# One encoder layer on one core: the small tables of the Fourier branch and of the rotation are loaded and split some column blocks later, and the first sum of folded weights is queued behind a low part on VectorE

## The chip, the core and the metric

The kernel runs on one core of a Trainium2 chip. Five engines work side by side, each through its own queue in order: TensorE (PE, matrix products and transposes; PEld is its load of the stationary operand), VectorE (DVE), ScalarE (ACT), GpSimd (POOL) and SyncE (SP), which here only issues transfers from and to main memory. The metric is the device time of one execution in microseconds, as the median of several runs.

## What is computed

One layer of a bidirectional encoder, 256 positions of 2048 channels, everything in float32:

```python
h = x + 0.5 * rms_post(swiglu(rms_pre(x)))            # first feed-forward half, width 5632
u = rms_pre(h);  q, k, v, f, g = split(u @ w_in)      # one projection for all of them
y_attn = gqa(rope(rms(q)), rope(rms(k)), v) @ w_attn_o   # 16 query heads, 4 key heads, 2-D rotation
y_four = real(fft2(f by groups of 128 channels)) @ w_fourier
merged = sigmoid(g_A) * y_attn + sigmoid(g_B) * y_four
h = h + rms_post(merged @ w_out)
y = h + 0.5 * rms_post(swiglu(rms_pre(h)))            # second half, same form
```

## The kernel before, in words

**Products in three passes.** Each float32 operand is split into a high part (a copy on ScalarE that rounds to the fast format, L104) and a low part (the difference, on VectorE, L105) by the helper `split` (L103). A product is three passes of TensorE: high by high (L110), high by low and low by high (L111, L112). So each weight goes through one ScalarE and one VectorE instruction before TensorE can use it. `split` notes the last two instructions that it made in `latest["A"]` and `latest["V"]`.

**How weights come.** A weight piece is 128 x 1024 elements (512 KB). It is loaded into one of 5 raw buffers (tag `raw`), split into one of 6 pairs of ring buffers (tags `hi`, `lo`), and used by 12 products: two blocks of 128 rows, two groups of 128 channels, three passes. Other small things share 8 buffers of the tag `wk`: temporary blocks, the rotation tables, the raw tables of the Fourier branch (`draw`, `mraw`), the gate bias `bg`, the sums `z`. Three buffers of the tag `xt` hold `z2` (sums of the Fourier branch), two tables (`alt`, `mid`), and later `acc` and `nraw`.

**Column blocks.** `col_block(u, w_in, nb, between, at)` computes 512 columns of the projection in 16 steps kk (one group of 128 channels each, 6 products per step), in four groups of two pieces. The entries of `between` are spread evenly: with n entries, entry i is called at the first step at or above (i + 1) * 16 / (n + 1). What it puts on TensorE is queued behind the product just made; its work on other engines isn't bound to that place.

**What sets the order.** The program is written once from top to bottom; the queue of each engine is then laid out when the program is built. An instruction is placed when a planner's estimate says that its inputs and its buffer are ready, earlier program text first. So a load or a split can be put well ahead of where it stands in the text. In the region of `last_rows` (the seam of two layers) the order on VectorE is written by hand among its own instructions. `tc.issue_after(ins)` puts what is written inside it, as far as it is on the engine of `ins`, behind `ins` in that engine's queue; it is an order, not a wait.

**The seam.** `last_rows` ends the first feed-forward half and begins the mixers: it adds the normed result to `h` (L405), multiplies by the next gain (L418, written `y`), transposes blocks of four (L180), splits them, and computes block 4 of `w_in` (the keys) between. Behind it, in program text, stand the loads of the rotation tables (`gq`, `gk`, `rc`, `rsn`) and of six tables of the Fourier branch: `dps` (256 positions, 128 x 258), `dcs` (channels, 128 x 256), `odd`, `first`, `alt`, `mid`; the first two are split, the other four are copied.

**The mixers.** Then follow in text: block 5 (values), gate 10, block 0 (first queries), gates 11, 12 and 13 (each a column block, a bias and a sigmoid). `fold_tokens` (L876) mirrors the token blocks with the row roots from `finish`, and `fold_f` (L932) takes 16 pieces of the Fourier projection during blocks 0, 11, 12, 13. `tables` (L831) multiplies the rotation tables by the gains; `norm_rope` uses them from gate 10 on. In gate 6 `fourier_positions` (`zh`, `zl`, reads `odd` and `dps`) and `fourier_channels` (reads `dcs`, `mid`, `alt`) come between steps, then `turn_q` for both blocks of queries. `fourier_weights(cb)` (L1106) takes four weight pieces: it adds two halves in the raw buffer (L1118), forms a difference (L1119), splits both, and sums a row over the four in `acc` (L1126, L1128), with factors from `fourier_channels`. `fourier_out` multiplies them (`pf`), after the attention scores (`sc`) and before the parts of attention.

Of the kernel before, what the change touches and what calls it, by code (L numbers as in the profile page):

```python
# [2 lines left out]

# [1 line left out]

# [10 lines left out]
ALU = mybir.AluOpType  # L16
# [42 lines left out]
def encoder_layer(  # L59
# [24 lines left out]
    def load(dst, src):  # L84
        nc.sync.dma_start(dst, src)
# [4 lines left out]
    def work(name, shape=None):  # L90
        return wk.tile(shape or [P, NB], F32, tag="wk", name=name)
# [11 lines left out]
    def split(hi, lo, src):  # L103
        a = A.activation(hi, src, AF.Copy)  # L104
        v = V.tensor_tensor(out=lo, in0=src, in1=hi.bitcast(F32), op=ALU.subtract)  # L105
        latest["A"], latest["V"] = a.ins, v.ins
# [714 lines left out]
        load(spill[t], h[t][:])  # L821

    gq, gk = work("gq", [P, HD]), work("gk", [P, HD])
    load(gq[:], q_g.partition_broadcast(P))
    load(gk[:], k_g.partition_broadcast(P))
    rc, rsn = work("rc", [P, NT, HD]), work("rsn", [P, NT, HD])
    load(rc[:], rope_cos)
    load(rsn[:], rope_sin)
    tabs = {}

    def tables():  # L831
        for nm, g in (("q", gq), ("k", gk)):
# [59 lines left out]
        ts = slice(t * P, (t + 1) * P)  # L892
        transpose4(kro[t], kT[:, 0, :, ts], kT[:, 1, :, ts])

    def constant(src, n):
        raw = work("draw", [P, n])
        load(raw[:], src)
        return raw

    WE, WO = P + 2, P  # L900
    dps = const.tile([P, 2, WE + WO], F32R, name="dps")
    split(dps[:, 0, :], dps[:, 1, :], constant(dft_pos, WE + WO)[:])
    dcs = const.tile([P, 2, 2 * P], F32R, name="dcs")
    split(dcs[:, 0, :], dcs[:, 1, :], constant(dft_ch, 2 * P)[:])
    odd = const.tile([P, WE], F32R, name="odd")
    A.activation(odd[:], constant(dft_ones[:, 0:WE], WE)[:], AF.Copy)
    first = const.tile([P, P], F32R, name="first")
    A.activation(first[:], constant(dft_ones[:, WE:WE + P], P)[:], AF.Copy)
    alt = xpool.tile([P, GROUPS // 2, NYR], F32R, tag="xt", name="alt")
    A.activation(alt[:].rearrange("p a b -> p (a b)"), constant(dft_ones[:, WE + P:], GROUPS // 2 * NYR)[:], AF.Copy)  # L910
    mid = xpool.tile([NS, 2 * P + 2 * NYR], F32R, tag="xt", name="mid")
    mraw = work("mraw", [NS, 2 * P + 2 * NYR])
    load(mraw[:], dft_mid)
    A.activation(mid[:], mraw[:], AF.Copy)


    fs, fraw = [], {}
# [80 lines left out]
    def fourier_channels(b, i, a):  # L998

        (ah, al), (oh, ol) = a  # L1000
        j = 2 * b + i
        if j == 0:
            foT.append(new_chunk("foT"))
            pmid[0] = ptr.tile([P, NB], F32, tag="tr", name="pn")
        pb = ptr.tile([P, NB], F32, tag="tr", name="pb")
        c = slice(i * WO, (i + 1) * WO)
        mm3(pb[:, 0:WO], dcs[0:PO, 0, P:2 * P], dcs[0:PO, 1, P:2 * P], oh[0:PO, c], ol[0:PO, c], True, True)
        c, m, o = slice(i * WE, (i + 1) * WE), slice(2 * WE, 3 * WE), pb[:, WO:WO + WE]
        mm3(o, dcs[0:PO, 0, 0:P], dcs[0:PO, 1, 0:P], ah[0:PO, c], al[0:PO, c], True, False)
        T.matmul(o, mid[:, i * P:(i + 1) * P], ah[0:NS, m], start=False, stop=False)  # L1010
        T.matmul(o, mid[:, i * P:(i + 1) * P], al[0:NS, m], start=False, stop=True)
        o = pmid[0][0:NYR, 0:WE]
        T.matmul(o, alt[0:PO, j, :], ah[0:PO, c], start=j == 0, stop=False)
        T.matmul(o, alt[0:PO, j, :], al[0:PO, c], start=False, stop=False)
        if i == 1:
            n = slice(2 * P + b * NYR, 2 * P + (b + 1) * NYR)
            T.matmul(o, mid[:, n], ah[0:NS, m], start=False, stop=False)
            T.matmul(o, mid[:, n], al[0:NS, m], start=False, stop=b == 1)
        split(foT[0][0][:, j, :], foT[0][1][:, j, :], pb[:, 0:2 * P])
        A.activation(dcol[:, j:j + 1], pb[:, 2 * P:2 * P + 1], AF.Copy)  # L1020
        if j == 3:
            A.activation(mids[0:NYR, :], pmid[0][0:NYR, 0:P], AF.Copy)
            V.tensor_tensor(out=mids[64:NYR, :], in0=pmid[0][64:NYR, 0:P], in1=mids[64:NYR, :].bitcast(F32), op=ALU.subtract)
            A.activation(dcol[0:GROUPS, 4:5], pmid[0][0:GROUPS, P:P + 1], AF.Copy)
# [69 lines left out]
    def gate(nb, dst, cb, between=(), at=()):  # L1094

        ps = col_block(u, w_in, nb, between=between, at=at)
        bg = work("bg")
        load(bg[:], b_gate[:, (nb - 6) * NB:(nb - 5) * NB].partition_broadcast(P))
        for t in range(NT):
            z = work("z")  # L1100
            V.scalar_tensor_tensor(out=z[:], in0=ps[t][:], scalar=rs[t][:, 0:1], in1=bg[:], op0=ALU.mult, op1=ALU.add)
            A.activation(cbs(dst[t], cb), z[:], AF.Sigmoid)
# [3 lines left out]
    def fourier_weights(cb):  # L1106


        acc = xpool.tile([P, NB], F32, tag="xt", name="acc")
        nraw, wn = xpool.tile([P, NB], F32, tag="xt", name="nraw"), workr("wn")  # L1110
        load(nraw[0:NYR, :], w_fn[cb])
        A.activation(wn[0:NYR, :], nraw[0:NYR, :], AF.Copy)
        V.tensor_tensor(out=wn[32:40, :], in0=nraw[32:40, :], in1=wn[32:40, :].bitcast(F32), op=ALU.subtract)
        forms = []
        for j in range(4):
            raw = wraw.tile([P, 2, NB], F32, tag="raw", name="raw")
            load(raw[:], w_fo[cb, j].rearrange("p (k c) -> p k c", k=2))
            V.tensor_tensor(out=raw[:, 0, :], in0=raw[:, 0, :], in1=raw[:, 1, :], op=ALU.add)  # L1118
            V.scalar_tensor_tensor(out=raw[:, 1, :], in0=raw[:, 1, :], scalar=-2.0, in1=raw[:, 0, :],  # L1119
                                   op0=ALU.mult, op1=ALU.add)  # L1120
            hi = wring.tile([P, 2, NB], F32R, tag="hi", name="whi")
            lo = wring.tile([P, 2, NB], F32R, tag="lo", name="wlo")
            split(hi[:], lo[:], raw[:])
            forms.append((hi, lo))
            if j == 0:
                V.tensor_scalar(out=acc[:], in0=raw[:, 0, :], scalar1=dcol[:, j:j + 1], scalar2=None, op0=ALU.mult)  # L1126
            else:
                V.scalar_tensor_tensor(out=acc[:], in0=raw[:, 0, :], scalar=dcol[:, j:j + 1], in1=acc[:],  # L1128
                                       op0=ALU.mult, op1=ALU.add)
        ready[cb] = acc, nraw, wn, forms  # L1130
# [21 lines left out]
            V.tensor_tensor(out=cbs(mB[t], cb), in0=w[:], in1=cbs(mB[t], cb), op=ALU.mult)  # L1152


    pv = col_block(u, w_in, 5, between=[nxt.finish, tables, lambda: fold_tokens(0)])
    for t in range(NT):
        vt = work("vt")
        A.activation(vt[:], pv[t][:], AF.Copy, scale=rs[t][:, 0:1])
# [7 lines left out]
    pq = col_block(u, w_in, 0, at=folds_at(4))  # L1166
    qs = []
    gate(11, mB, 1, at=folds_at(4), between=[lambda t=t: qs.append(norm_rope(pq, "q", t)) for t in range(NT)])
    gate(12, mB, 2, at=folds_at(4), between=[lambda t=t: turn_k(t) for t in range(NT)])
    gate(13, mB, 3, at=folds_at(4))  # L1170

    yA, zA = ([big(f"{n}{t}") for t in range(NT)] for n in ("yA", "zA"))
    mT = []
# [210 lines left out]
```

## Time and profile before

| | |
|---|---|
| median of 3 runs | 2004.93 us (2003.99 to 2006.01) |
| profiled execution | 2006.3 us |
| its span, first to last instruction | 2004.2 us |
| PE busy | 1984.0 us (99%) |
| DVE busy | 1780.1 us (89%) |
| ACT busy | 1301.2 us (65%) |
| mean granted clock of PE | 0.997 |

The profile is of one execution. Times in its rows are microseconds from the start of the span. A row of the timeline has start, duration, engine (SPq is SyncE's issue of transfers), line, operation, output<-input with buffer numbers left out, sizes and count; a bracket at its end gives the idle time before it and what ended it. A row of the windows has a stretch and its length, then busy time and instructions of PE, PEld, DVE, ACT and POOL, then the granted clock of PE (1.00 is full), the share of the transfer engines' time, and GB/s. A row of waits has the waiting engine and instruction, what it waited for, total, times and longest.

### The profile page before, as it was taken

The numbers are of one execution on the slowest core, as the hardware profiler recorded it, in microseconds if no ns is written. First come the engines' busy times: TensorE is split into PE (matmuls) and PEld (weight loads), VectorE is DVE, ScalarE is ACT, GpSimd is POOL, SyncE is SP. The second block draws the span as 40 slices with busy tenths as digits, with TensorE's granted clock in tenths as the row PEclk, the third lists the DMA queues.
The fourth block names the chain that finished last, engine by engine and source line by source line (L and its number), as shares of the span: only waits on it lengthen the run. The fifth ranks groups of instructions, "written<-read, shape, count | busy, mean of one in ns | idle before, by whom it ended". The sixth has DMA issues, their size and how long they took to land.

```text
span 2004.2 us, 25805 instructions
## 1 busy us (share of the span) xinstructions
PE 1984.0 (99%) x9146; PEld 1644.8 (82%) x9146; DVE 1780.1 (89%) x2352; ACT 1301.2 (65%) x1860; POOL 84.5 (4%) x94
## 2 busy tenths in 40 slices
PE   9999999999999999999999999999999999999998
PEld 7888888888888878888888888878888888888886
DVE  6899999999999878886877885878999999999996
ACT  7566766767667756556666564656677766677666
POOL 0000000000000000100000000000000000000002
PEclk9999999999999999999999999999999999999999
DMA  8657766677668796954555557565577766677673
GB/s 319 211 175 240 225 232 199 200 249 228 226 204 275 250 280 201 261 184 138 195 189 188 192 166 277 194 215 194 169 236 231 231 210 208 213 233 229 208 264 126
DMA packets 117585, 434.20 MB, mean 217 GB/s; under 512 B 12840, under 2 KB 18992, under 8 KB 106064
## 3 DMA queue, kind: packets, MB, share of 16 engines
q1 hardware_dynamic: 103888, 411.65, 59.9%
q0 software_dynamic: 13568, 20.91, 6.0%
q8 instruction: 71, 1.16, 0.2%
q14 instruction: 58, 0.48, 0.1%
HBM read 409.44 MB, written 6.29 MB: 207 GB/s over the span
## 4 chain that ended last, share of the span: by engine, by line
PE 90%; DVE 5%; DMA 3%; ACT 1%; issue 1%; SPq 0%; DVEq 0%; ACTq 0%
PE pc L111 18%; PE pc L112 18%; PE pc L110 18%; PE pr L112 10%; PE pr L111 10%; PE pr L110 10%; DVE wlo L105 2%; PE pt L180 1%; DMA raw<-in_f_gu 1%; DMA raw<-in_w_fo 1%; DVE t L582 0%; PE pe L110 0%; PE pe L112 0%; PE pe L111 0%; PE pt L1072 0%
## 5 line engine op out<-in xcount | busy, mean ns | idle before, releaser
L105 DVE TENSOR_TENSOR wlo<-raw,whi 128x1024 fp32r<-128x1024 f32 (+1 forms) x567 | 681.1, 1219 | 96.9 <-ACT whi L104 95.2
L104 ACT ACTIVATE whi<-raw 128x1024 fp32r<-128x1024 f32 (+1 forms) x567 | 585.8, 1052 | 253.7 <-PE pc L112 109.3
L111 PE MATMUL pc<-wlo,fh 128*128 128x512 f32 x738 | 287.3, 389 | 0.0
L112 PE MATMUL pc<-whi,fl 128*128 128x512 f32 x738 | 287.3, 389 | 0.0
L110 PE MATMUL pc<-whi,fh 128*128 128x512 f32 x738 | 287.1, 389 | 0.0
L110 PE MATMUL pc<-whi,uh 128*128 128x512 f32 x688 | 271.7, 395 | 1.5 <-ACT uh L786 1.5
L111 PE MATMUL pc<-wlo,uh 128*128 128x512 f32 x688 | 269.8, 392 | 1.7 <-DVE wlo L105 1.7
L112 PE MATMUL pc<-whi,ul 128*128 128x512 f32 x688 | 269.6, 392 | 0.0
L104 ACT ACTIVATE whi<-t 128x1024 fp32r<-128x1024 f32 (+1 forms) x198 | 171.6, 867 | 139.4 <-DVE t L582 130.8
L582 DVE TENSOR_TENSOR t<-raw 128x512 f32<-128x512 f32 (+1 forms) x252 | 209.1, 842 | 14.1 <-DMA raw<-in_f_gu 10.3
L110 PE MATMUL pr<-whi,hTh 128*128 128x512 f32 x544 | 213.4, 392 | 0.0
L112 PE MATMUL pr<-whi,hTl 128*128 128x512 f32 x544 | 211.8, 389 | 0.0
L111 PE MATMUL pr<-wlo,hTh 128*128 128x512 f32 x544 | 211.7, 389 | 0.0
L105 DVE TENSOR_TENSOR wlo<-t,whi 128x1024 fp32r<-128x1024 f32 (+1 forms) x198 | 193.6, 978 | 13.4 <-ACT whi L104 13.0
L104 ACT ACTIVATE w<-raw 128x1024 fp32r<-128x1024 f32 x144 | 152.0, 1055 | 40.8 <-DVE raw L582 34.7
L105 DVE TENSOR_TENSOR w<-raw,w 128x1024 fp32r<-128x1024 f32 x144 | 175.6, 1219 | 0.0
L111 PEld LDWEIGHTS pc<-wlo,fh 128*128 128x128 f32 x738 | 138.5, 188 | 29.2 <-DVE wlo L105 0.3
L110 PEld LDWEIGHTS pc<-whi,fh 128*128 128x128 f32 x738 | 138.5, 188 | 28.9
L112 PEld LDWEIGHTS pc<-whi,fl 128*128 128x128 f32 x738 | 138.5, 188 | 28.7
L111 PEld LDWEIGHTS pc<-wlo,uh 128*128 128x128 f32 x688 | 129.8, 189 | 28.5 <-DVE wlo L105 3.6
L110 PEld LDWEIGHTS pc<-whi,uh 128*128 128x128 f32 x688 | 129.7, 188 | 28.5 <-ACT uh L786 2.8
L112 PEld LDWEIGHTS pc<-whi,ul 128*128 128x128 f32 x688 | 129.6, 188 | 27.0
(360 smaller groups left out, 3188.4 us busy)
## 6 DMA issues: line engine op xcount, KB each, us to landing
raw<-in_f_down SPq DMA_DIRECT2D x176, 512.0 KB, 5.0
raw<-in_f_gu SPq DMA_DIRECT2D x144, 512.0 KB, 4.8
raw<-in_f_gu SPq DMA_DIRECT2D x72, 1024.0 KB, 7.0
raw<-in_w_in SPq DMA_DIRECT2D x112, 512.0 KB, 4.5
raw<-in_f_up SPq DMA_DIRECT2D x32, 512.0 KB, 4.5
raw<-in_w_ao SPq DMA_DIRECT2D x32, 512.0 KB, 3.8
raw<-in_w_out SPq DMA_DIRECT2D x32, 512.0 KB, 4.5
raw<-in_f_gate SPq DMA_DIRECT2D x31, 512.0 KB, 5.8
```

The costliest lines, as they stand in the source:

```text
L104: a = A.activation(hi, src, AF.Copy)
L105: v = V.tensor_tensor(out=lo, in0=src, in1=hi.bitcast(F32), op=ALU.subtract)
L110: T.matmul(ps, lh, rh, start=first, stop=False, skip_group_check=onto)
L111: T.matmul(ps, lh, rl, start=False, stop=False, skip_group_check=onto)
L112: return T.matmul(ps, ll, rh, start=False, stop=last, skip_group_check=onto)
L180: T.transpose(pt[:, j, :], src[:, j * P:(j + 1) * P], ident[:])
L582: V.tensor_tensor(out=out, in0=a, in1=b, op=ALU.subtract)
```

## The change

The four loads of the rotation tables move into a function `rotation`, called in block 5 as its second entry; `tables` goes from the second to the fifth of now five entries, `fold_tokens(0)` stays third. With five entries the steps are 3 (`finish`), 6 (`rotation`), 8 (`fold_tokens(0)`) and 14 (`tables`), where they were 4 (`finish`), 8 (`tables`) and 12 (`fold_tokens(0)`).

The six Fourier tables are loaded by `ask` and split or copied by `take`: `alt`, `mid`, `first` in gate 12 (steps 8 and 14, behind the two `turn_k`, which go from steps 6 and 11 to 3 and 6), `dps`, `odd`, `dcs` in gate 13 (steps 4 and 12). `alt` and `mid` get their buffers only then.

The sum of the first folded weight piece (L1118, for cb 0 and j 0 alone) is queued on VectorE behind `latest["V"]`. At that place of the text this is the low part that `turn_q` made last in gate 6 (`qTl` of the second block).

```diff
     gq, gk = work("gq", [P, HD]), work("gk", [P, HD])
-    load(gq[:], q_g.partition_broadcast(P))
-    load(gk[:], k_g.partition_broadcast(P))
     rc, rsn = work("rc", [P, NT, HD]), work("rsn", [P, NT, HD])
-    load(rc[:], rope_cos)
-    load(rsn[:], rope_sin)
     tabs = {}
+
+    def rotation():
+        load(gq[:], q_g.partition_broadcast(P))
+        load(gk[:], k_g.partition_broadcast(P))
+        load(rc[:], rope_cos)
+        load(rsn[:], rope_sin)
...
-    def constant(src, n):
-        raw = work("draw", [P, n])
-        load(raw[:], src)
-        return raw
-
     WE, WO = P + 2, P
     dps = const.tile([P, 2, WE + WO], F32R, name="dps")
-    split(dps[:, 0, :], dps[:, 1, :], constant(dft_pos, WE + WO)[:])
     dcs = const.tile([P, 2, 2 * P], F32R, name="dcs")
-    split(dcs[:, 0, :], dcs[:, 1, :], constant(dft_ch, 2 * P)[:])
     odd = const.tile([P, WE], F32R, name="odd")
-    A.activation(odd[:], constant(dft_ones[:, 0:WE], WE)[:], AF.Copy)
     first = const.tile([P, P], F32R, name="first")
-    A.activation(first[:], constant(dft_ones[:, WE:WE + P], P)[:], AF.Copy)
-    alt = xpool.tile([P, GROUPS // 2, NYR], F32R, tag="xt", name="alt")
-    A.activation(alt[:].rearrange("p a b -> p (a b)"), constant(dft_ones[:, WE + P:], GROUPS // 2 * NYR)[:], AF.Copy)
-    mid = xpool.tile([NS, 2 * P + 2 * NYR], F32R, tag="xt", name="mid")
-    mraw = work("mraw", [NS, 2 * P + 2 * NYR])
-    load(mraw[:], dft_mid)
-    A.activation(mid[:], mraw[:], AF.Copy)
+    late = {}
+
+    def ask(*names):
+
+        srcs = {"dps": dft_pos, "dcs": dft_ch, "odd": dft_ones[:, 0:WE], "first": dft_ones[:, WE:WE + P],
+                "alt": dft_ones[:, WE + P:], "mid": dft_mid}
+        for n in names:
+            raw = work("draw", list(srcs[n].shape))
+            load(raw[:], srcs[n])
+            late[n] = raw
+
+    def take(*names):
+
+        for n in names:
+            raw = late[n]
+            if n in ("dps", "dcs"):
+                dst = {"dps": dps, "dcs": dcs}[n]
+                split(dst[:, 0, :], dst[:, 1, :], raw[:])
+            elif n in ("odd", "first"):
+                A.activation({"odd": odd, "first": first}[n][:], raw[:], AF.Copy)
+            elif n == "alt":
+                late[n] = xpool.tile([P, GROUPS // 2, NYR], F32R, tag="xt", name="alt")
+                A.activation(late[n][:].rearrange("p a b -> p (a b)"), raw[:], AF.Copy)
+            else:
+                late[n] = xpool.tile([NS, 2 * P + 2 * NYR], F32R, tag="xt", name="mid")
+                A.activation(late[n][:], raw[:], AF.Copy)
...
             load(raw[:], w_fo[cb, j].rearrange("p (k c) -> p k c", k=2))
-            V.tensor_tensor(out=raw[:, 0, :], in0=raw[:, 0, :], in1=raw[:, 1, :], op=ALU.add)
+            with tc.issue_after(latest["V"]) if cb == 0 and j == 0 else nullcontext():
+                V.tensor_tensor(out=raw[:, 0, :], in0=raw[:, 0, :], in1=raw[:, 1, :], op=ALU.add)
...
-    pv = col_block(u, w_in, 5, between=[nxt.finish, tables, lambda: fold_tokens(0)])
+    pv = col_block(u, w_in, 5, between=[nxt.finish, rotation, lambda: fold_tokens(0), None, tables])
...
-    gate(12, mB, 2, at=folds_at(4), between=[lambda t=t: turn_k(t) for t in range(NT)])
-    gate(13, mB, 3, at=folds_at(4))
+    gate(12, mB, 2, at=folds_at(4), between=[lambda t=t: turn_k(t) for t in range(NT)]
+         + [lambda: ask("alt", "mid", "first"), None, lambda: take("alt", "mid", "first")])
+    gate(13, mB, 3, at=folds_at(4), between=[lambda: ask("dps", "odd", "dcs"), None, lambda: take("dps", "odd", "dcs")])
```

More of the change, by code (lines that the diff above doesn't have):

```diff
@@ L1 @@
 import math
-from contextlib import ExitStack
+from contextlib import ExitStack, nullcontext
 import numpy as np
@@ L1009, in fourier_channels @@
         mm3(o, dcs[0:PO, 0, 0:P], dcs[0:PO, 1, 0:P], ah[0:PO, c], al[0:PO, c], True, False)
-        T.matmul(o, mid[:, i * P:(i + 1) * P], ah[0:NS, m], start=False, stop=False)
-        T.matmul(o, mid[:, i * P:(i + 1) * P], al[0:NS, m], start=False, stop=True)
+        T.matmul(o, late["mid"][:, i * P:(i + 1) * P], ah[0:NS, m], start=False, stop=False)
+        T.matmul(o, late["mid"][:, i * P:(i + 1) * P], al[0:NS, m], start=False, stop=True)
         o = pmid[0][0:NYR, 0:WE]
-        T.matmul(o, alt[0:PO, j, :], ah[0:PO, c], start=j == 0, stop=False)
-        T.matmul(o, alt[0:PO, j, :], al[0:PO, c], start=False, stop=False)
+        T.matmul(o, late["alt"][0:PO, j, :], ah[0:PO, c], start=j == 0, stop=False)
+        T.matmul(o, late["alt"][0:PO, j, :], al[0:PO, c], start=False, stop=False)
         if i == 1:
             n = slice(2 * P + b * NYR, 2 * P + (b + 1) * NYR)
-            T.matmul(o, mid[:, n], ah[0:NS, m], start=False, stop=False)
-            T.matmul(o, mid[:, n], al[0:NS, m], start=False, stop=b == 1)
+            T.matmul(o, late["mid"][:, n], ah[0:NS, m], start=False, stop=False)
+            T.matmul(o, late["mid"][:, n], al[0:NS, m], start=False, stop=b == 1)
         split(foT[0][0][:, j, :], foT[0][1][:, j, :], pb[:, 0:2 * P])
```

## The prediction

> **What bounds the kernel now.** I read the page first, then busy time by stretches of the span, then who waited for whom, then the order in time of each engine around the two places that this picked out.
>
> ```profile
> span 2004.2 us, 25805 instructions
> PE 1984.0 (99%) x9146; PEld 1644.8 (82%) x9146; DVE 1780.1 (89%) x2352; ACT 1301.2 (65%) x1860; POOL 84.5 (4%) x94
> ```
>
> TensorE is busy 1984.0 of 2004.2 us. Only its pauses, and stretches at a lower clock, can be won. Two lie beside lines that the diff touches (columns: PE, PEld, DVE, ACT and POOL busy, granted clock, DMA share, GB/s):
>
> ```profile
> 690.00:720.00 30.00, 26.34 (x120) 21.07 (x119) 25.01 (x55) 16.59 (x40) 4.39 (x4) 0.94 0.80 230
> 880.00:925.00 45.00, 43.46 (x231) 36.44 (x230) 30.40 (x44) 20.61 (x36) 0.00 (x0) 0.96 0.40 131
> 709.09:719.38 10.29, 6.63 (x23) 4.59 (x22) 7.64 (x12) 4.75 (x13) 0.59 (x1) 0.83 0.94 251
> 892.94:897.54 4.60, 3.08 (x23) 2.94 (x22) 3.53 (x6) 1.44 (x2) 0.00 (x0) 0.81 0.57 188
> 909.66:911.67 2.01, 2.01 (x22) 2.01 (x21) 0.72 (x1) 1.45 (x2) 0.00 (x0) 1.00 0.00 0
> 895.70:899.50 3.80, 3.80 (x19) 3.46 (x18) 3.73 (x6) 1.08 (x3) 0.00 (x0) 0.55 0.49 166
> ```
>
> PE lacks 3.7 us in the first stretch (30.00 less 26.34) and 1.5 in the second (45.00 less 43.46), and the granted clock falls to 0.55 in parts of them. The waits name the cause:
>
> ```profile
> ACT dps L104 <- DMA draw<-in_dft_pos: 8.3, 1, 8.3
> DVE dps L105 <- ACT dps L104: 2.4, 1, 2.4
> PE pt L180 <- DVE y L418: 2.5, 1, 2.5
> PE pa L979 <- DVE zl L105: 1.5, 1, 1.5
> ```
>
> ScalarE stands 8.3 us before the table `dft_pos`, VectorE 2.4 us behind ScalarE, and TensorE 2.5 us behind the product that VectorE could not start. The 1.5 us belong to the second place.
>
> **First part: the tables at the seam of the two layers.** In order of time, SyncE, DVE and PE:
>
> ```profile
> 705.85 0.47 SPq L85 DMA_DIRECT2D draw<-in_dft_pos  x1
> 708.94 1.22 DVE L105 TENSOR_TENSOR wlo<-raw,whi 128x1024 fp32r<-128x1024 f32 x1
> 710.08 0.75 DVE L405 SCALAR_TENSOR_TENSOR h<-y,cr,h 128x512 f32<-128x512 f32 x1
> 713.20 0.43 DVE L105 TENSOR_TENSOR dps<-draw,dps 128x258 fp32r<-128x258 f32 x1 [2.38 <-ACT dps L104]
> 713.54 0.69 DVE L418 TENSOR_TENSOR y<-h,gpre 128x512 f32<-128x512 f32 x1
> 707.05 0.39 PE L110 MATMUL pc<-whi,uh 128*128 128x512 f32 x1
> 709.09 0.39 PE L110 MATMUL pc<-whi,uh 128*128 128x512 f32 x1
> 710.22 0.50 PE L111 MATMUL pc<-wlo,uh 128*128 128x512 f32 x1 [0.74 <-DVE wlo L105]
> 714.38 0.63 PE L180 MATMUL pt<-ident,y 128*128 128x128 f32 x4 [2.50 <-DVE y L418]
> 719.38 0.60 PE L180 MATMUL pt<-ident,y 128*128 128x128 f32 x4
> ```
>
> From 707.05 to 709.09 there are nine steps of PE, 0.227 us each. From 709.09 to 719.38 stand 18 such products and one group of four transposes (0.60 us at most, by the 719.38 row): 18 x 0.227 + 0.60 = 4.7 us of work in 10.29. So 5.6 us are lost. Not all comes back. The first gap (709.09 to 710.22, 0.9 us over one step) waits for a low part that started at 708.94 on a VectorE with nothing idle before it; it stays. Without `dps` in its queue VectorE goes from `h` (start 710.08, 0.75) to `y`: it starts at about 710.8, 2.7 us sooner, and ends at 711.5. PE comes to the transposes after six products from 710.22, at 711.6 to 711.7, and finds `y` done. The low part behind `y` ends at 711.4 + 1.22 = 712.6, while the transposes end at 712.3: a pause of 0.3 us stays. Eleven products later PE is at 712.6 + 2.5 = 715.1, plus 0.1 for the restart, instead of 719.38. **Saved: 4.2 us.** Bounds: 2.7 (only VectorE's start moves, the low clock stays) to 5.6 (all of it).
>
> What is late next is VectorE itself: it has `ul`, two more `h`, `y` pairs in front of the later transposes, by 0.69 to 0.75 us each, which leaves PE 0.2 to 0.5 us at each of them by my count; I put nothing down for it.
>
> Where the moved work goes. Ten loads leave SyncE around 705.85, so weight loads that stand behind them move up. The four rotation tables go to step 6 of block 5, their twelve small products on VectorE (the first is the 733.08 row, none has more elements, so under 3.4 us together) from step 8 to step 14, and folding of token block 0 from step 12 to step 8, that is 24 products or 5.4 us sooner in PE's order. That fold needs the roots, which `finish` (a step earlier now) makes:
>
> ```profile
> 733.08 0.28 DVE L837 TENSOR_TENSOR gcq<-rc,gq 128x128 f32<-128x128 f32 x1
> 737.65 0.74 DVE L881 SCALAR_TENSOR_TENSOR uo<-y,r1r,ua 128x512 f32<-128x512 f32 x1
> 746.64 0.60 PE L886 MATMUL pt<-ident,ue 128*128 128x128 f32 x4
> ```
>
> Transposes at 746.64 become 746.64 - 5.4 - 4.2 = 737.0. The second operand ended at 738.4; 4.2 us sooner, and not counting that the tables leave its front, it ends at 734.2. So 2.8 us are in hand: cost 0. If that cover were gone, each microsecond beyond it would cost PE one. The six tables of the Fourier branch go into gates 12 and 13, where a table is asked for 6 steps (gate 12) or 8 steps (gate 13) before ScalarE takes it; a gate is 27 us for 16 steps there, so 10 and 13 us by these rows:
>
> ```profile
> 863.10 0.75 DVE L1101 SCALAR_TENSOR_TENSOR z<-pc,r0r,bg 128x512 f32<-128x512 f32 x1
> 863.60 0.42 SPq L85 DMA_DIRECT2D bg<-in_b_gate  x1
> 890.16 0.74 DVE L1101 SCALAR_TENSOR_TENSOR z<-pc,r0r,bg 128x512 f32<-128x512 f32 x1
> 892.43 0.41 ACT L104 ACTIVATE zh<-zs 128x260 fp32r<-128x260 f32 x1
> ```
>
> (863.10 to 890.16 is gate 13.) In the old place `dft_pos` took 713.20 - 705.85 = 7.3 us from issue to VectorE, a copy on ScalarE included. The tables are first read behind 892.43, 9 us after the take at about 883. ScalarE and VectorE split ring pieces ahead there; the two splits and four copies, under 0.45 us each by `dps` above, cost 0. If that cover fails, ScalarE holds the weight splits behind it up again.
>
> **Weighing a rule.** Behind a pause of 1.5 us the clock stood at 0.55 for 3.80 us, and the mean of 0.83 over the 10.29 us says the same of the pause of 2.5 us. The slow clock goes with the pause. The Trainium skill, "TensorE: Matmul & The Clock Gate" (Part 1: The HAM clock gate), has the clock fall only after about 3.4 us without work. By that rule neither pause brings its slow stretch with it, and 10.29 x 0.17 + 3.80 x 0.45 = 3.5 us would stay, which makes the sum 3.1 us. The trace disagrees, and I take the trace.
>
> **Second part: the first sum of folded weights.** One group of the page, then in order of time the loads, the queue of VectorE, and TensorE behind it:
>
> ```profile
> L104 ACT ACTIVATE whi<-raw 128x1024 fp32r<-128x1024 f32 (+1 forms) x567 | 585.8, 1052 | 253.7 <-PE pc L112 109.3
> ...
> 889.14 7.96 SPq L85 DMA_DIRECT2D raw<-in_w_fo  x4
> 920.15 31.92 SPq L85 DMA_DIRECT2D raw<-in_w_in  x13
> 891.52 1.23 DVE L105 TENSOR_TENSOR wlo<-raw,whi 128x1024 fp32r<-128x1024 f32 x1
> 893.98 0.69 DVE L1118 TENSOR_TENSOR raw<-raw 128x512 f32<-128x512 f32 x1 [1.23 <-DMA raw<-in_w_fo]
> 894.59 0.42 DVE L105 TENSOR_TENSOR zl<-zs,zh 128x260 fp32r<-128x260 f32 x1
> 895.06 0.33 PE L979 MATMUL pa<-odd,zl 128*126 128x130 f32 x1 [1.51 <-DVE zl L105]
> 919.62 0.48 DVE L1126 TENSOR_SCALAR acc<-raw,dcol 128x512 f32<-128x512 f32 x1
> 926.64 0.69 DVE L105 TENSOR_TENSOR qTl<-pt,qTh 128x512 fp32r<-128x512 f32 x1
> 929.35 0.40 PE L110 MATMUL pf<-whi,foTh 128*128 128x512 f32 x1
> 935.91 0.39 PE L110 MATMUL pc<-whi,uh 128*128 128x512 f32 x1
> ```
>
> The sum on L1118 waits 1.23 us for its DMA, and `zl`, ready since `zh` (892.43 + 0.41), stands behind it. Without that `zl` ends at 893.3, when PE asks for it. The block of TensorE takes 4.60 us here and 2.01 the second time: 2.6 us; the products behind it run at 0.55 of the clock until 899.50 and lose about (899.50 - 897.54) x 0.45, some 0.8 more. **Saved: 3.4 us**, bounds 1.5 (the pause alone) and 3.4.
>
> The price lies later. The sum now queues behind the last split traced before it, `qTl` of the second token tile, at 926.64: 33 us later. Behind it on VectorE come its difference, the low part, and the whole chain `acc`, which was done from 919.62 on. The order of all four weights' products starts with this one. By rows: `qTl` ends at 927.3, two `z` (0.74 each) go first, sum and difference 2 x 0.69 to 930.1, high part on ScalarE 1.05 (the group's mean) to 931.2, low part 1.23: 932.4. PE wants the high part at 929.35. So 2 to 3 us must be covered by other work. The next block's first piece of 12 products (12 x 0.227 = 2.7 us) can: its load went out long before (loads go out in the order of use, and those from 920.15 on are the pieces after it), and as it was run from 935.91 on, it can be drawn forward. Behind that, four of the five raw buffers come free only with the `acc` chain, at 931 to 934 instead of from 919.62 on, and the second piece is wanted at about 938.6; a load took 4.8 us from issue to use here (889.14 to 893.98), and a split 2.3: 938 to 941. I take **1 us lost**. Bounds: 0 (cover holds) and 5 (2.7 for the product, 2.3 for the piece); a gain is excluded, since nothing is taken off that stretch.
>
> **The sum.** 4.2 + 3.4 - 1.0 = 6.6 us. The profiled execution took 2006.3 us, 2.1 around the span of 2004.2; its span becomes 1997.6. The median of the runs, 2004.93, lies 1.4 below the profiled execution, and becomes 1998.3. With the bounds (gain of 2.7 + 1.5 + 0 less 5, against 5.6 + 3.4) the outer ends are 2005.7 and 1995.9; likely is 1996.5 to 2001.
>
> **The rivals.**
> *Another sum takes its place* (0.13). Only the first of four sums is held back. The second one, from a load issued about 1.1 us later, may now be queued before `zl`, and the pause stays as long or longer. Against it: `zl` was placed right behind the first sum, so it was ready by then. Gain 4.2 - 1 = 3.2: 2001.7.
> *The tables are loaded where they were* (0.10). A load has no inputs; it could go out whenever a buffer is free, wherever it stands in the text, and its split with it. For: SyncE is free there. Against: `bg` at 863.60 went out only behind the `z` that used the one before (863.10), though buffers of its kind were free, so they are given in order of the text. Gain 3.4 - 1 = 2.4: 2002.5.
> *The late sum starves the next block* (0.09), the slower side. If the planner places the four attention maxima before the `acc` chain, four raw buffers stay shut until about 940, loads land at 944, and splits are done at 947, where PE is through at 938.6: 8 us of pause and 2 of low clock, against 7.6 won: 2007.3. It decides from a first load later than about 937 on.
> *A wait in gates 12 and 13 or at the fold* (0.08). A table's split stands on ScalarE before it has landed, for 2 to 4 us that the ring doesn't cover, with the clock: gain 3 to 4, 2001.5. The Trainium skill, "DMA: Bandwidth & Descriptors" (Rules for kernel authors), has a load issued early and awaited late; by it the new places are the worse ones. The row of `dft_pos` speaks the other way: it was awaited for 8.3 us in the old one.
>
> **How the numbers follow.** Forecast 0.60 at 1998.3. The range 1995.5 to 2003.5 takes in its bounds and all rivals but the starved one and the worst ends. A measurement of this kernel can tell about 0.2%, or 4 us, from no change (its three runs lie 2 us apart), so faster means below 2000.9: nearly all of the forecast and some of the edge cases, 0.65. Same: the rivals at 2001 to 2003, 0.26. Slower: 0.09.
>
> **What would show it.** Right: no `dps` split near 705 to 715, PE from the product at 709.09 to the third transposes in about 6 us at full clock; `zl` directly behind `zh`; the sum on L1118 behind `qTl`. Wrong: a wait of ACT for `draw` before or inside gates 12 and 13 that PE feels; a pause of PE between the attention scores and `pf`, or before the next block's second piece, by over 3 us; the second sum in front of `zl`.

## The result and the profile after

The changed kernel takes 2009.36 us (median of 16 runs, 2007.15 to 2011.94), the kernel before 2005.53 (16 runs, 2003.00 to 2008.46): a ratio of 1.0018, 95% interval 1.0011 to 1.0025. It is slower by 0.18%, some 3.6 us, which is just inside what the prediction called no change; the forecast was 6.6 us faster, and the time lies outside its range. The profiled execution took 2008.8 us.

The head of its page, then the same stretches by busy time, of the kernel after first and of the kernel before second (two of them were not shown yet):

```profile
span 2006.7 us, 25805 instructions
PE 1984.2 (99%) x9146; PEld 1644.1 (82%) x9146; DVE 1779.1 (89%) x2352; ACT 1299.5 (65%) x1860; POOL 85.1 (4%) x94
```

```profile
690.00:720.00 30.00, 28.91 (x142) 22.99 (x141) 27.88 (x66) 17.02 (x40) 5.46 (x5) 1.00 0.84 266
837.00:890.00 53.00, 51.26 (x266) 43.39 (x265) 42.01 (x47) 29.05 (x36) 2.19 (x2) 1.00 0.66 204
880.00:925.00 45.00, 43.21 (x239) 36.08 (x238) 23.26 (x36) 15.57 (x32) 0.00 (x0) 1.00 0.38 125
925.00:940.00 15.00, 12.06 (x50) 9.51 (x49) 14.94 (x23) 12.45 (x21) 0.00 (x0) 0.77 0.42 145
```

```profile
837.00:890.00 53.00, 53.00 (x280) 45.32 (x278) 42.59 (x47) 28.92 (x32) 2.19 (x2) 1.00 0.65 212
925.00:940.00 15.00, 15.00 (x81) 12.64 (x80) 11.93 (x20) 12.50 (x27) 0.00 (x0) 1.00 0.62 213
```

At the seam the long pause and the slow clock are gone, as forecast. Two stretches that were full in the kernel before now have holes: gates 12 and 13 (51.26 of 53.00) and the stretch around `pf` (12.06 of 15.00, at a clock of 0.77).

To put a price on each, take one landmark for each gate, the start of its first `z` on VectorE. For the kernel before they are 787.26 (gate 10), 837.44 (11), 890.16 (13), 927.25 (6) and 1146.75 (9), and its last product starts at 1994.05. The table gives the difference to the kernel before, stage by stage, in the one profiled execution of every kernel; the letters are those of the experiments below.

| us against the kernel before | up to gate 10 (seam) | 10 to 11 | 11 to 13 | 13 to 6 | 6 to 9 (`pf`) | 9 to the end | sum |
|---|---|---|---|---|---|---|---|
| **after** | -3.96 | +0.30 | **+2.38** | -1.26 | **+7.00** | -1.57 | +2.89 |
| A tables moved, no sum held | -3.59 | -0.04 | +2.08 | +0.29 | +0.40 | -1.94 | -2.80 |
| B sum held, no table moved | +0.10 | +0.07 | 0.00 | +0.08 | +7.50 | -0.76 | +6.99 |
| C held piece last | -3.80 | -0.08 | +3.31 | +1.93 | +0.61 | -1.96 | +0.01 |
| D held piece last, buffers shut | -3.00 | -0.01 | +2.28 | -1.05 | +4.39 | -1.78 | +0.83 |
| E sums behind `ol` | -4.18 | +0.01 | +3.62 | -2.94 | +0.23 | -1.89 | -5.15 |
| F takes tied | -2.83 | +0.48 | 0.00 | +0.58 | +6.41 | -1.96 | +2.68 |
| G = E and F | -3.65 | +0.32 | -0.01 | -2.93 | +0.07 | -1.96 | -8.16 |
| H sums behind `ol`, no table moved | +0.66 | +0.13 | 0.00 | -2.99 | +0.15 | -0.67 | -2.72 |
| I takes tied, no sum held | -3.64 | -0.24 | +0.04 | +0.56 | +0.11 | -1.91 | -5.08 |
| J only the rotation moved | +1.97 | +0.14 | +0.01 | -1.33 | +0.01 | -0.69 | +0.11 |
| K = G, `frest` in the next buffer | -1.84 | +0.08 | -0.01 | -2.88 | +0.03 | -0.68 | -5.30 |
| L longer `xt` buffers, no table moved | -1.11 | +0.41 | 0.00 | +0.07 | +0.19 | -0.68 | -1.13 |

One execution carries noise, at the seam above all. L's edit doesn't touch it, and it differs there by 1.11 us (its pause before the transposes is 1.28 us, in the kernel before 2.50, in H 2.88). Kernels whose seam is written alike (after, A, C to G, I, K) spread from -1.84 to -4.18. So a difference of 1 to 2 us in that column means nothing by itself; the larger losses in the others are read beside the pauses in the rows.

**The seam of the kernel after**, DVE and then PE in order of time:

```profile
709.94 0.75 DVE L405 SCALAR_TENSOR_TENSOR h<-y,cr,h 128x512 f32<-128x512 f32 x1
710.60 0.15 DVE L439 TENSOR_REDUCE tot<-ssn 128x1 f32<-128x4 f32 x1
710.72 0.69 DVE L418 TENSOR_TENSOR y<-h,gpre 128x512 f32<-128x512 f32 x1
```

```profile
711.57 0.62 PE L180 MATMUL pt<-ident,y 128*128 128x128 f32 x4
712.60 0.50 PE L111 MATMUL pc<-wlo,uh 128*128 128x512 f32 x1 [0.42 <-DVE wlo L105]
```

No split of `dps` stands between `h` and `y`, and TensorE comes to its transposes with nothing to wait for.

**Gates 12 and 13**: SyncE's load of `alt` in gate 12, then ScalarE in both gates, then TensorE in both.

```profile
834.28 0.42 SPq L85 DMA_DIRECT2D draw<-in_dft_ones  x1
```

```profile
840.58 0.45 ACT L924 ACTIVATE alt<-draw 128x288 fp32r<-128x288 f32 x1 [3.66 <-DMA draw<-in_dft_ones]
841.36 1.04 ACT L104 ACTIVATE whi<-raw 128x1024 fp32r<-128x1024 f32 x1
869.18 0.42 ACT L104 ACTIVATE dps<-draw 128x258 fp32r<-128x258 f32 x1 [2.89 <-DMA draw<-in_dft_pos]
```

```profile
847.87 0.39 PE L111 MATMUL pe<-wlo,ueh 128*128 128x260 f32 x1 [0.87 <-DVE wlo L105]
876.54 0.39 PE L111 MATMUL pe<-wlo,ueh 128*128 128x260 f32 x1 [0.87 <-DVE wlo L105]
```

The copy of `alt` is written six steps behind its load, but it was queued right behind it: it stands 3.66 us at the head of ScalarE's queue, and the weight split that starts at 841.36 stands behind it.

**Gate 6 and `pf`**: VectorE, then ScalarE, then TensorE, then SyncE.

```profile
891.58 0.43 DVE L105 TENSOR_TENSOR zl<-zs,zh 128x260 fp32r<-128x260 f32 x1
894.46 0.69 DVE L1132 TENSOR_TENSOR raw<-raw 128x512 f32<-128x512 f32 x1 [2.45 <-DMA raw<-in_w_fo]
898.55 0.40 DVE L105 TENSOR_TENSOR ol<-pa,oh 126x256 fp32r<-126x256 f32 x1
924.10 0.69 DVE L105 TENSOR_TENSOR qTl<-pt,qTh 128x512 fp32r<-128x512 f32 x1 [2.52 <-ACT qTh L104]
926.86 0.69 DVE L1132 TENSOR_TENSOR raw<-raw 128x512 f32<-128x512 f32 x1
928.07 0.68 DVE L1133 SCALAR_TENSOR_TENSOR raw<-raw 128x512 f32<-128x512 f32 x1
```

```profile
898.61 1.04 ACT L104 ACTIVATE whi<-raw 128x1024 fp32r<-128x1024 f32 x1
...
928.78 3.90 ACT L104 ACTIVATE whi<-raw 128x1024 fp32r<-128x1024 f32 x4 [2.00 <-DVE raw L1133]
...
934.91 2.00 ACT L104 ACTIVATE whi<-raw 128x1024 fp32r<-128x1024 f32 x2
```

```profile
898.45 0.33 PE L110 MATMUL pb<-oh,dcs 126*128 126x128 f32 x1 [1.42 <-ACT oh L104]
...
926.70 0.28 PE L112 MATMUL sc<-kT,qTl 128*128 128x256 f32 x1
929.89 1.22 PE L110 MATMUL pf<-whi,foTh 128*128 128x512 f32 x2 [2.91 <-ACT whi L104]
```

```profile
902.27 0.33 SPq L85 DMA_DIRECT2D raw<-in_w_in  x1
...
931.13 26.56 SPq L85 DMA_DIRECT2D raw<-in_w_in  x14
```

The first sum is held until 926.86, as it was meant to be. But no weight at all is split between 898.61 and 928.78: the other three pieces, summed from 894 on, are split behind the held one (the four in one row), and the next block's first piece, whose load went out at 902.27, is split only at 934.91. In the kernel before ScalarE splits seven weights in this time, the first and the last of them here:

```profile
901.34 1.06 ACT L104 ACTIVATE whi<-raw 128x1024 fp32r<-128x1024 f32 x1 [1.29 <-PE pc L112]
...
927.45 1.06 ACT L104 ACTIVATE whi<-raw 128x1024 fp32r<-128x1024 f32 x1 [0.84 <-PE pc L112]
```

In the kernel after TensorE has nothing to do for 2.91 us, and the clock falls behind it:

```profile
929.00:931.00 2.00, 1.11 (x2) 0.50 (x2) 2.00 (x4) 2.00 (x3) 0.00 (x0) 0.62 0.00 0
931.00:933.00 2.00, 1.96 (x5) 1.49 (x5) 2.00 (x3) 1.98 (x3) 0.00 (x0) 0.50 0.34 106
933.00:935.00 2.00, 2.00 (x6) 1.58 (x5) 2.00 (x3) 1.99 (x6) 0.00 (x0) 0.50 0.85 305
935.00:937.00 2.00, 2.00 (x7) 1.58 (x7) 2.00 (x5) 2.00 (x4) 0.00 (x0) 0.68 0.94 336
```

### The profile page after: what moved, and what is told of

The parts are those of the page before. It is cut to its first block, busy times and chain, and to the rows that moved or that the text cites. A ratio compares the mean times of both kernels' runs of the same rounds, so it can differ in the third digit from the quotient of the medians.

```text
span 2006.7 us, 25805 instructions
## 1 busy us (share of the span) xinstructions
PE 1984.2 (99%) x9146; PEld 1644.1 (82%) x9146; DVE 1779.1 (89%) x2352; ACT 1299.5 (65%) x1860; POOL 85.1 (4%) x94
## 4 chain that ended last, share of the span: by engine, by line
PE 90%; DVE 5%; DMA 2%; ACT 1%; issue 1%; SPq 0%; DVEq 0%; ACTq 0%
PE pc L111 18%; PE pc L112 18%; PE pc L110 18%; PE pr L110 10%; PE pr L112 10%; PE pr L111 10%; DVE wlo L105 2%; PE pt L180 1%; DMA raw<-in_w_fo 1%; ACT whi L104 1%; DMA raw<-in_w_in 1%; DMA raw<-in_f_gu 0%; PE pf L110 0%; PE pf L111 0%; PE pf L112 0%
```

## The experiments

The theory: the ring pairs are given out in the order of the program text, so one held split holds every split behind it; that and the slow clock are the loss at `pf`. The takes, queued right behind their loads, are the loss in gates 12 and 13. The seam won what was forecast. Rivals: the late raw buffers are the cause, or the moved tables are. Ratios are to the kernel before, with their 95% intervals.

**A. The moved tables alone**; the sum stands as before. Against the kernel after:

```diff
-            with tc.issue_after(latest["V"]) if cb == 0 and j == 0 else nullcontext():
-                V.tensor_tensor(out=raw[:, 0, :], in0=raw[:, 0, :], in1=raw[:, 1, :], op=ALU.add)
+            V.tensor_tensor(out=raw[:, 0, :], in0=raw[:, 0, :], in1=raw[:, 1, :], op=ALU.add)
```

> The moved tables alone; the first sum is queued where it was before the change. Theory (the held sum keeps the other splits behind it waiting, and that is the loss): the seam gives its 4.0 us, gates 12 and 13 keep the 2.7 us that the late tables cost there, so the time is about 1.3 us below the kernel before (ratio near 0.9993); the pause in front of zl (1.5 us) and its slow stretch are back, and there is no pause of 2.9 us at pf. Rival (the loss comes from the moved tables): the time stays near that of the changed kernel, 3 to 4 us above the kernel before.

Measured 0.9991 (0.9982 to 1.0001), 1.8 us below, with an interval that just reaches no change. The pause at `zl` is back (1.76 us, with a slow stretch); there is none at `pf`. The loss at `pf` doesn't come from the tables; the one in gates 12 and 13 is still there (2.08).

**B. The held sum alone**; all tables stay at the seam. Against the kernel before:

```diff
-            V.tensor_tensor(out=raw[:, 0, :], in0=raw[:, 0, :], in1=raw[:, 1, :], op=ALU.add)
+            with tc.issue_after(latest["V"]) if cb == 0 and j == 0 else nullcontext():
+                V.tensor_tensor(out=raw[:, 0, :], in0=raw[:, 0, :], in1=raw[:, 1, :], op=ALU.add)
```

> The held sum alone; all tables are loaded where they were before the change. Theory: gate 6 gains 1.3 us, the stretch from z of gate 6 to z of gate 9 loses about 6.9, so the time is about 5.6 us above the kernel before (ratio near 1.0028), with the pause of about 2.9 us at pf and a slow clock behind it. Rival (the loss comes from the moved tables): no slower than the kernel before, 0 to 3 us below it.

Measured 1.0027 (1.0016 to 1.0037), 5.4 us above, with a pause of 2.92 us at `pf`. The held sum is the whole loss there. Gate 6, where 1.3 us of gain was expected, gives none (+0.08).

**C. The held piece last**, still held behind the same `qTl`; the order of the products and of `acc` follows. Against the kernel after:

```diff
-        forms = []
-        for j in range(4):
+        forms, behind = [], latest["V"]
+        order = [1, 2, 3, 0] if cb == 0 else [0, 1, 2, 3]
+        for j in order:
...
-            with tc.issue_after(latest["V"]) if cb == 0 and j == 0 else nullcontext():
+            with tc.issue_after(behind) if cb == 0 and j == 0 else nullcontext():
...
-            if j == 0:
+            if j == order[0]:
...
```

> The changed kernel with the held weight piece taken last of the four: its sum is still queued behind the same qTl, but the splits of the three others stand ahead of it. Theory (a split that stands behind a held one in the text waits for it): the pause at pf is 0.5 us or less and the clock is full from 925 to 937, while the first sum that is not held stands in front of zl again with its pause of 1.5 us; gain at pf 6.9, loss at zl 1.3: some 5.6 us below the changed kernel, 1.8 below the kernel before. Rival (any late sum starves the raw buffers or crowds VectorE): the pause only moves to the last of the four pieces or to the second piece of the next block, and the time stays 2 us or more above the kernel before.

Measured 1.0002 (0.9993 to 1.0011), 0.4 us above, where 1.8 below was expected. At `pf` it went as the theory says: the row of this kernel has no slow clock, and gate 6 to gate 9 loses 0.61 us in place of 7.00.

```profile
925.00:940.00 15.00, 14.72 (x77) 11.95 (x76) 10.98 (x20) 9.66 (x20) 0.00 (x0) 1.00 0.33 108
```

What I had too low is the pause at `zl`: 1.83 us here, with a slow stretch of twice the usual length behind it (1.93 lost from gate 13 to 6). Gates 12 and 13 lose 3.31 in place of 2.38, with one more pause, of 0.52 us.

**D. The same, but `acc` begins with the held piece**, so that the raw buffers of the other three stay shut. Against C:

```diff
...
             forms.append((hi, lo))
-            if j == order[0]:
+            raws[j] = raw
+        for j in range(4):
+            raw = raws[j]
+            if j == 0:
```

> As the run before, but the chain acc still begins with the held piece, so all four raw buffers stay shut until about 928 as in the changed kernel. Theory (the splits' order is the cause, not the buffers): as the run before within 1 us, no pause at pf. Rival (late buffers starve the next block): raw loads go out near 931 as in the changed kernel, a pause of 2 us or more comes before a product of the next block, and the time is 2 us or more above the kernel before.

Measured 1.0018 (1.0009 to 1.0027), 3.6 us above. Here the theory fell: the splits are early, `pf` doesn't wait, and yet gate 6 to gate 9 loses 4.39 us. The rival had the time and the late loads right (they go out at 930.76; in C at 921.50), but not the one pause of 2 us or more. TensorE waits in pieces, the largest of them 50 us on, where the kernel before waits 0.40:

```profile
935.88 0.50 PE L111 MATMUL pc<-wlo,uh 128*128 128x512 f32 x1 [0.97 <-DVE wlo L105]
942.75 0.44 PE L1085 MATMUL pt<-ident,p 128*128 128x128 f32 x2 [0.77 <-ACT p L1074]
990.16 0.66 PE L180 MATMUL pt<-ident,o 128*128 128x128 f32 x4 [1.63 <-DVE o L869]
```

So the held sum has a second cost beside the splits that wait behind it. What makes it up isn't separated: D brings the raw buffers late (a split at 937.64 waits 1.05 us for its load) and with them the chain `acc`, and the low part in front of the 935.88 row, which starts at 934.62, stands on a VectorE that has been busy almost without a break since 924.87. In the kernel after this cost must for the most part hide behind the first, since the pause of 2.91 us and the slow clock behind it come near the whole 7.00 there. No run has late splits with early buffers: a split can't read its raw buffer before the sum.

**E. All four sums behind `ol`**, the last low part that the first `fourier_positions` needs, and none behind `qTl`. Against the kernel after:

```diff
         split(oh[0:PO, :], ol[0:PO, :], po[0:PO, 0:2 * WO])
+        marks.setdefault("ol", latest["V"])
...
-            with tc.issue_after(latest["V"]) if cb == 0 and j == 0 else nullcontext():
+            with tc.issue_after(marks["ol"]) if cb == 0 else nullcontext():
```

> The changed kernel, but all four sums of the first fourier_weights are queued behind the last low part of fourier_positions (ol, near 898.6) and none behind qTl. Theory (what zl needs is that no sum stands in front of it or of al and ol; what pf needs is that no sum waits for qTl): the pause of zl, the one of 1.4 us at oh, and the one at pf are all gone; 8 to 9 us below the changed kernel, about 4.7 below the kernel before (ratio near 0.9977). Rival (the sums must run early, in the wait for zl, or their buffers come late): loads of the next block go out later than 922, a pause of over 1 us comes before pf or the next block, and the gain on the changed kernel is under 5 us.

Measured 0.9977 (0.9968 to 0.9986), 4.6 us below. The pauses at `zl`, at `oh` and at `pf` are gone, and gate 6 gives 2.94. Gates 12 and 13 still lose, 3.62 in the profiled execution, a slow stretch included.

**F. The takes tied** behind the split that was written before them on ScalarE. Against the kernel after:

```diff
+    def bound(*names):
+        with tc.issue_after(latest["A"]):
+            take(*names)
...
-         + [lambda: ask("alt", "mid", "first"), None, lambda: take("alt", "mid", "first")])
+         + [lambda: ask("alt", "mid", "first"), None, lambda: bound("alt", "mid", "first")])
```

(and the same in gate 13)

> The changed kernel with the splits and copies of the six Fourier tables tied in ScalarE's queue behind the last split written before them, so that they run several us later than their loads. Theory (a split placed right behind its load holds ScalarE for 3.7 and 2.9 us, and that costs 2.7 us in gates 12 and 13): ScalarE's waits for draw fall under 0.5 us, the pauses of 0.9 us in both gates go, and the time is 2.7 us below the changed kernel, about 1 above the kernel before. Rival (ScalarE's wait is hidden, the 2.7 us are something else in these gates, such as the eight-buffer pool or VectorE): the waits for draw go, the pauses stay, no change within 1 us.

Measured 1.0006 (0.9997 to 1.0015), 1.2 us above, that is 2.4 below the kernel after by the ratios, where 2.7 was expected; the two intervals overlap a little. `alt` is copied 15 us after its load (835.58 to 850.60), without a wait, and gates 11 to 13 lose nothing. So the 2.38 us were ScalarE's wait. The profiled execution shows almost none of the gain (+2.68 against +2.89), because in it the seam gives 1.1 us less and the pause at `oh` is longer (1.66 us) and has a slow stretch behind it (+0.58 from gate 13 to 6, where the kernel after has -1.26).

**G. Both edits, E and F.**

> The two edits before this one together: sums behind ol, and the tables' splits tied behind the splits written before them. Theory: the seam's 4.0 and gate 6's 3.4 us are both won with nothing lost, about 7.4 us below the kernel before (ratio near 0.9963) and 11 below the changed kernel. Rival (something else than these two waits takes the gain back): under 4 us below the kernel before.

Measured 0.9961 (0.9949 to 0.9974), 7.8 us below the kernel before: 1998.15 us (median of 5 runs). The three places in this kernel:

```profile
837.00:890.00 53.00, 52.87 (x275) 44.98 (x274) 43.96 (x49) 31.18 (x41) 2.19 (x2) 1.00 0.69 216
880.00:925.00 45.00, 44.84 (x254) 37.79 (x253) 33.86 (x49) 22.68 (x40) 0.00 (x0) 1.00 0.51 163
925.00:940.00 15.00, 15.00 (x74) 12.17 (x73) 10.19 (x18) 14.97 (x34) 0.00 (x0) 1.00 0.54 176
```

TensorE is full or nearly so at a clock of 1.00 in all of them. The seam and gate 6 give 3.65 and 2.93 us, near the 4.2 and 3.4 that were forecast for the change; in the change the order of the sum and the place of the takes gave them back. Another 1.96 comes behind gate 9 (K and L).

**H. Edit E on the kernel before**, no table moved; the diff is that of E.

> The kernel before, with the one edit that all four sums of the first fourier_weights are queued behind ol; no table is moved. Theory (the two parts of the change add up, and each wins what its place lost): gate 6 gives the 3.4 us of the pause at zl and of its slow stretch, the seam keeps its pauses, so about 3.4 us below the kernel before (ratio near 0.9983). Rival (the sums' place only pays once the tables are out of the way): within 1 us of the kernel before.

Measured 0.9984 (0.9976 to 0.9993), 3.2 us below.

**I. The moved tables with edit F**, no sum held; the diffs are those of A and F.

> The moved tables with their splits and copies tied behind the splits written before them on ScalarE; no sum is held. Theory: the seam gives its 4.0 us and gates 12 and 13 give nothing back, so about 4 us below the kernel before (ratio near 0.9980), 2.7 below the run of the moved tables alone; the pause of 1.5 us in front of zl stays. Rival (the seam's gain is lost elsewhere on the way): as the run of the moved tables alone, 1 to 2 us below the kernel before.

Measured 0.9974 (0.9964 to 0.9985), 5.2 us below, and 3.4 below A. The two parts add up: 3.2 and 5.2 are 8.4, G measured 7.8.

**J. Only the rotation tables moved.** Against the kernel before, beside the function `rotation` of the change:

```diff
-    pv = col_block(u, w_in, 5, between=[nxt.finish, tables, lambda: fold_tokens(0)])
+    pv = col_block(u, w_in, 5, between=[nxt.finish, rotation, lambda: fold_tokens(0), None, tables])
```

> The kernel before, with only the rotation tables moved into block 5 (rotation, fold and tables at their new steps); the six Fourier tables stay at the seam. Theory (the seam's pause comes from dps, whose split holds ScalarE and through it VectorE): the wait of about 8 us for draw and the pause of about 2.5 us before the transposes stay, the time is within 1 us of the kernel before. Rival (the ten loads in SyncE's queue are the cause, or the fold at its earlier step costs): 2 us or more below, by the four loads that leave the queue, or 1 us or more above, with a new pause at the fold.

Measured 0.9990 (0.9981 to 0.9999), 2.0 us below; I had put it within 1, and 2 is the figure of the rival. In the trace the mechanism is the one expected, at another place: ScalarE stands 5.48 us before `dps`, VectorE behind it, and now a low part stands behind both, for which TensorE waits longer than before:

```profile
710.69 0.43 DVE L105 TENSOR_TENSOR dps<-draw,dps 128x258 fp32r<-128x258 f32 x1 [1.61 <-ACT dps L104]
711.94 0.43 DVE L105 TENSOR_TENSOR dcs<-draw,dcs 128x256 fp32r<-128x256 f32 x1 [0.75 <-ACT dcs L104]
712.93 1.22 DVE L105 TENSOR_TENSOR wlo<-raw,whi 128x1024 fp32r<-128x1024 f32 x1
```

```profile
714.20 0.79 PE L111 MATMUL pc<-wlo,uh 128*128 128x512 f32 x1 [3.98 <-DVE wlo L105]
```

The profiled execution shows no gain (+0.11 in the table). Where the 2 us of the medians come from stays open, and so does whether the four loads that left the queue have a part in it.

**K and L. The buffer of `frest`.** All kernels with moved Fourier tables win 1.6 to 2.0 us after gate 9, the other three 0.7 to 0.8, though no pause of 0.5 us or more lies there in any trace. The second feed-forward half has 108 products whose stationary operand is `frest`, a tile of the tag `xt`, whose three buffers `alt` and `mid` now take at another time. The page's groups from 1200 us on, first the kernel before, then the one after:

```profile
L110 PE MATMUL pc<-whi,frest 128*128 128x512 f32 x36 | 14.2, 396 | 0.0
```

```profile
L110 PE MATMUL pc<-whi,frest 128*128 128x512 f32 x36 | 14.0, 389 | 0.0
```

K takes one more `xt` buffer in kernel G ahead of `frest`; L makes the `xt` buffers of the kernel before longer.

```diff
+                        spare = xpool.tile([P, 4, P], F32R, tag="xt", name="spare")
+                        V.tensor_copy(out=spare[:, 0, 0:1], in_=ident[:, 0:1])
                         rest = xpool.tile([P, 4, P], F32R, tag="xt", name="frest")
```

```diff
-            xt = xpool.tile([P, 2, S + 1], F32, tag="xt", name="xt")[:, 0:n, :]
+            xt = xpool.tile([P, 2, S + 8], F32, tag="xt", name="xt")[:, 0:n, 0:S + 1]
```

> The fastest version so far (sums behind ol, tables' splits tied), with one more buffer of the tag xt taken, and one column written to it, just before the piece frest of the second feed-forward half gets its buffer, so that frest falls on the next of the three. The question is why the 108 products that read frest take 396 ns each wherever the Fourier tables stay at the seam and 389 ns wherever they are moved. Theory (it depends on which of the three buffers frest has, and the moved tables changed that): 396 ns in this run, or, if two of the three buffers are alike, 389 again. Rival (it depends on something else that the tables change): 389 ns. So 396 decides for the theory, 389 leaves it open. The time is within 2 us of 1998.

> The kernel before, with the three xt buffers made a little longer (2112 bytes a partition in place of 2080), so that all three start at the same place within 64 bytes. Theory (a buffer's start within 64 bytes sets it): 389 ns for the products that read frest, 1 us less from gate 9 to the end, everything ahead as in the kernel before. Rival (it is not where the buffer starts): 396 ns, nothing changes.

K, one execution of 2000.6 us: 396 ns again, and gate 9 to the end is 846.62 us, where G has 845.34. So it is which of the three buffers `frest` has, worth 1.3 us by these two executions. The time itself was expected within 2 us of 1998 and lies 0.6 beyond: K's seam stage gives 1.84 where G's gives 3.65, which the edit doesn't touch. L, one execution of 2004.8 us: the three groups of products that read `frest` take 395 to 397 ns, no change. That the buffers' spacing within 64 bytes sets it is not borne out; why one buffer is read more slowly stays open. The other 0.7 us behind gate 9 every kernel wins, K and L too, so it belongs to the one execution of the kernel before.

## Why the prediction was wrong

*The seam: right.* 4.2 us were forecast, 3.96 measured, though one execution tells this column only to 1 or 2 us; `y` started at 710.72 (forecast 710.8), the transposes at 711.57 (711.6 to 711.7), and the pause behind them was 0.42 (0.3). The fold's transposes started at 737.25 (forecast 737.0), and no pause stands in front of them: the cover held. (The +0.30 from gate 10 to 11 is a pause of 0.29 us at 825.04, in gate 11.) The Trainium skill, "TensorE: Matmul & The Clock Gate" (Part 1: The HAM clock gate), lets the clock fall after a whole idle window of about 3.4 us; against it, the slow stretch went with the pause of 2.50 us, as the prediction took from the trace.

*The failing step: the cover at `pf`.* The prediction saw that the first piece comes 2 to 3 us late (2.91 measured) and let "the next block's first piece of 12 products" cover it, since its load "went out long before". The load did, at 902.27; the split did not (934.91). The step took the order of loads for the order of splits. The split rows of the kernel after come in text order, and run C shows that putting the held piece last removes the pause; whether it is the ring pairs or ScalarE's queue that keeps this order, no run separates. The second thing missing was the clock: from 929.89 to about 936.3 TensorE ran at 0.50 (the four rows above), which is another 3.2 us. The third, late buffers, was in the sum with bounds of 0 to 2.3; in run D, where the pause at `pf` is gone, they and the late `acc` cost 4.39 together. Put at 1 with bounds of 0 to 5, the step cost 7.00: 2.91 of pause, 3.2 of clock, and 0.9 behind them, 0.6 of which is a longer pause in front of the transposes of `o` (1.01 us at 991.99, 0.40 in the kernel before).

*The takes in gates 12 and 13: wrong.* Cost 0 rested on 6 and 8 steps between load and take. Nothing binds a take to its step: what isn't on TensorE may be queued as soon as the planner holds it for ready, and the copy stands in the queue right behind its load, before the data had landed. The rival "A wait in gates 12 and 13 or at the fold", given 0.08, came true in its first half, beside the loss at `pf`: ScalarE waits 3.66 and 2.89 us, as it said, 2.38 are lost, and run F takes them away. The Trainium skill, "DMA: Bandwidth & Descriptors" (Rules for kernel authors), asks for an early load and a late wait. That is a rule on the distance between the two, not, as the prediction read it, against the new places; runs F and I agree: the late wait was the part that the change had in its text and not in its queue.

*Gate 6: half right.* `zl` now stands directly behind the low part before it, as forecast, and its pause is gone. But 3.4 us became 1.26: the second sum waits 2.45 us for its load at the head of VectorE's queue, `al` stands behind it, `oh` on ScalarE behind a copy that waits 3.87 us for `al`, and TensorE pauses 1.42 us at `oh`. The prediction had that rival ("another sum takes its place") and looked for it only in front of `zl`. B has the same pause (1.18 us) with a slow stretch behind it, and gains nothing there.

*The sum.* Forecast -4.2 - 3.4 + 1.0. Measured -3.96, +0.30, +2.38, -1.26, +7.00, and -1.57 behind gate 9, which nobody had in view (the buffer of `frest`, and the execution of the kernel before): +2.89 in the profiled execution.

## What to carry to other kernels

An order that holds one instruction back can hold everything that is handed out behind it: before it is given, follow not only that engine's queue but every buffer that is given out in program order, to the first consumer that finds nothing. Tie it to the last thing that has to go first (here `ol`) and not to a thing that is merely later (`qTl`, 25 us on). A late load is only half of a move; the instruction that takes the data has to be tied to its new place too, or a scheduler puts it right behind the load and the wait comes along.

## What the runs showed of the hardware

A pause of TensorE doesn't cost its length alone, and what it costs beside it isn't set by its length. Behind pauses of 1.18 (B), 1.51 (kernel before), 1.66 (F) and 1.76 us (A) the clock fell to 0.50; behind 1.42 (after), 1.43 and 1.63 (D), 1.81 and 1.84 us (both in B) it stayed at 1.00. In E a pause of 0.62 and one of 0.87 us, 0.4 apart, were enough. Where the slow stretches begin falls on a grid. These are the first slow slices of 0.2 us of two stretches, in the kernel before and in F:

```profile
714.80:715.00 0.20, 0.20 (x2) 0.00 (x0) 0.20 (x1) 0.00 (x0) 0.00 (x0) 0.77 0.68 138
895.80:896.00 0.20, 0.20 (x4) 0.20 (x2) 0.20 (x1) 0.00 (x0) 0.00 (x0) 0.53 0.46 184
```

```profile
899.80:900.00 0.20, 0.20 (x2) 0.12 (x1) 0.20 (x1) 0.00 (x0) 0.00 (x0) 0.76 0.45 174
930.60:930.80 0.20, 0.14 (x1) 0.14 (x1) 0.20 (x2) 0.20 (x2) 0.00 (x0) 0.56 0.00 0
```

A mean of 0.77 over 0.20 us at a clock of 1.00 and then 0.50 puts the fall at 714.91; likewise 895.81, 899.90 and 930.62. The distances are 180.90 and 30.72 us, which are 53 and 9 times 3.413. The Trainium skill, "TensorE: Matmul & The Clock Gate" (Part 1: The HAM clock gate), has a free-running window of 3413 ns, and the runs agree with it; that a window has to be idle as a whole, as the same page has it, they don't.

The grid also fits the one pair of like pauses with unlike ends. The first row is E's first slow slice behind its two pauses, the second C's first slow slice of the trace:

```profile
849.00:849.20 0.20, 0.20 (x4) 0.20 (x3) 0.20 (x1) 0.20 (x1) 0.00 (x0) 0.55 0.74 142
895.00:895.20 0.20, 0.20 (x3) 0.20 (x3) 0.20 (x1) 0.00 (x0) 0.00 (x0) 0.61 0.55 225
```

The falls are at 849.02 and 895.04. E's window from 845.61 to 849.02 holds both pauses, 1.49 us together. C has them too (0.52 and 0.87 us, ending at 847.11 and 848.37), but 14 windows ahead of 895.04 is 847.26: a border of the grid lies between them, and the clock stayed. That is one pair, not a rule: B's window from 711.30 to 714.72 (55 windows ahead of its fall at 902.45) is idle for 1.75 us, and the clock stayed there too. A stretch lasts one window, or two (kernel after, C, J), and costs up to 1.7 or 3.4 us of work. What in a window decides wasn't measured by itself and stays open.
